# Hybrid decoder trunk: the seven products of a column pair interleaved with those of the next, one weight tile per product, residual added in memory by DMA

## The chip, the core and the metric

The kernel runs on one core of a Trainium2 chip. The metric is the device time of one execution in microseconds (us): the median of three runs, and beside it the time of one execution that the hardware profiler recorded. A core has TensorE (PE, its weight loads PEld), VectorE (DVE), ScalarE (ACT), GpSimd (POOL) and SyncE (SP), each with an in-order queue of its own, and 16 DMA engines that serve the transfers which SP, POOL and ACT issue.

## What is computed

One layer on 2048 tokens of width 1024 in fp32. Three causal mixers share an input and an output projection; behind them stand a gated MLP with a causal convolution of width 3 over the tokens, a per-layer embedding with a gate, and a final RMSNorm. The change lies in the MLP and at its two edges. Cut to that:

```
x = x + y @ w_out                              # y: outputs of the three mixers
h = rmsnorm(x, norm_ffn_gain)
gu = causal_dwconv(h @ ffn_w_up, ffn_conv_w)   # width 3, 2 * 2816 columns
g, u = split(gu, 2)
x = x + (silu(g) * u) @ ffn_w_down             # 2816 -> 1024
gate = sigmoid(x @ ple_w_gate)
x = x + gate * (p @ ple_w_proj)
out = rmsnorm(x, final_norm_gain)
```

## The kernel before

The tokens are worked in two halves of 1024 (`TH`), each of two chunks of 512 (`CH`, `NC` = 2). Features lie on the 128 partitions (`P`), so `x` is eight tiles `x[m]` of 128 x 1024. Each half goes through the mixers, the output projection, the MLP and the embedding; the code is written out in the order in which each engine works it off.

Every fp32 product is three matmuls (`mm3`): each operand is split in a high part, rounded by a copy on ACT (L196), and a low part, the difference taken by DVE (L197). L203 multiplies high by high, L204 the low part of the tokens by high weights, L205 the high tokens by low weights. A matmul takes 128 x 128 weights and 512 tokens.

The MLP has 22 column blocks `j` (`NJ`), each of 128 gate columns (`zg`) and 128 up columns (`zu`). For `j` = 0, `up_first` makes 8 plain products (a product: `KQ` = 4 row blocks of 128, 12 matmuls, one PSUM bank of 128 x 512). For `j` ≥ 1, `up` makes 7 products, a scheme that saves the eighth by sums of weights and of tokens. They are called p1 to p7 after the tokens that they use (`X[1]` to `X[7]`, tiles `h`, split once at the start of the MLP). p1, p6, p7 and p4 accumulate in one bank `pa` (`A`), p5 and p3 in one half of `pbc` (`B`), p2 alone in the other (`Cc`). The running sums are wanted in between, so ACT copies a bank out before the next product adds to it: L849 copies `pa` to `zg` after p1, L857 `pbc` to `zu` after p5, L861 `pa` to `zg` after p6, L894 `pa` to `zu` after p4. Where a product only has to be added to such a copy, DVE does it.

After the products of `j` come the convolutions (`conv_g`, `conv_u`: L344 on ACT, L348 twice on DVE), silu on ACT (L803), the multiply (L808) and the split in `ahi` and `alo` on ACT and DVE. The order of the products is p1, p5, p6, p2, p7, p3, p4 for odd `j` and p1, p2, p5, p6, p3, p7, p4 for even `j`. For even `j`, between the gate's convolution and p4, stands a down-projection group (`down`): two earlier blocks of the activations, times their rows of `w_down`, into all 1024 output features, 16 banks `pdn` of two `j` each (96 matmuls); DVE adds each bank into `x` (L907). The last two blocks follow at the end, one by one. I call two `j` and their group a pair.

Weights arrive on SP's queue as tiles `wr` of 512 KB, two at a time (`wp`), each split by the job that uses it. `w_get` runs the jobs of the list `wlist` two ahead of the one wanted. In the output projection ahead of the MLP GpSimd's queue loads `xr`, the residual, which DVE adds to each bank `po`. For the second half the sums of squares of its `x` are taken ahead of time, during the first half's MLP (`nstats`).

Of the kernel before, what the change touches and what calls it, by code (L numbers as in the profile page):

```python
# [9 lines left out]
F32 = mybir.dt.float32  # L10
# [38 lines left out]
def trunk(ctx, tc, xT, pT, w_in, w_out, w_up, w_down, w_pp, w_pg, wr_bd, wi_bd, vecs, consts, masks, out):  # L49
# [70 lines left out]

    raws = {}

    def job_a(hf, j):
        g = raws[hf, j, 0] = raw_w(kc(w_up[j]))
        raws[hf, j, 1] = raw_w(kc(w_up[NJ + j]))
        hi, lo = ftile("wh", F32R), ftile("wl", F32R)
        split(hi, lo, g)
        return hi, lo

    def job_u(hf, j):  # L130
        hi, lo = ftile("wh", F32R), ftile("wl", F32R)
        split(hi, lo, raws[hf, j, 1])
        return hi, lo

    def job_s(hf, j, which):
        g, u = raws[hf, j, 0], raws[hf, j, 1]
        hi, lo = ftile("wh", F32R), ftile("wl", F32R)
        q = [slice(0, CH), slice(CH, D)]
        if which == 0:

            s = raws[hf, j, 2] = sp.tile([P, D], F32, tag="s", name=nm("s"), bufs=1)
            TT(s[:, q[0]], u[:, q[0]], u[:, q[1]], op=ADD)
            TT(s[:, q[1]], s[:, q[0]], g[:, q[0]], op=SUB)
        else:

            s = raws[hf, j, 2]
            TT(s[:, q[0]], g[:, q[1]], s[:, q[1]], op=SUB)
            TT(s[:, q[1]], g[:, q[0]], u[:, q[0]], op=SUB)
        split(hi, lo, s)
        return hi, lo  # L150

    def job_a22(hf, j):
        t = ftile("w22", F32R)
        split(t[:, :CH], t[:, CH:], raws[hf, j, 1][:, CH:])
        return t

    def job_d(hf, js, m0, per):
        return whole(w_down[m0 : m0 + per, :, js[0] : js[-1] + 1, :].rearrange("m p j c -> p m (j c)"), ftile)
# [3 lines left out]
    for hf in range(NH):  # L162
        wlist += [(("in", hf, m), lambda m=m: whole(kc(w_in[m]), t4)) for m in IN_UNITS]
        wlist += [(("out", hf, c, m), lambda m=m: whole(kc(w_out[m]), t4)) for c in range(NC) for m in range(KD)]
        for j in range(NJ):
            a = (hf, j)
            if j == 0:
                wlist += [(("a", *a), lambda a=a: job_a(*a)), (("u", *a), lambda a=a: job_u(*a))]
                continue
            wlist += [(("a", *a), lambda a=a: job_a(*a))]  # L170
            wlist += [(("s", *a, i), lambda a=a, i=i: job_s(*a, i)) for i in range(2)]
            down = [(("d", hf, j // 2 - 1, i), lambda a=hf, js=GROUPS[j // 2 - 1], i=i: job_d(a, js, 4 * i, 4)) for i in range(2)]
            if j % 2 == 0:
                wlist.append(down[0])
            wlist.append((("a22", *a), lambda a=a: job_a22(*a)))
            if j % 2 == 0:
                wlist.append(down[1])
        wlist += [(("d", hf, gi, 0), lambda a=hf, js=GROUPS[gi]: job_d(a, js, 0, 8)) for gi in range(len(GROUPS) - 2, len(GROUPS))]
        wlist += [(("pg", hf, t, m), lambda m=m: whole(kc(w_pg[m]), t4)) for t in range(len(ple_chunks(hf == NH - 1))) for m in range(KD)]
    wat = {key: i for i, (key, _) in enumerate(wlist)}  # L180
    wmade = {}
    wpos = [0]

    def w_upto(n):
        while wpos[0] < min(n, len(wlist)):
            key, job = wlist[wpos[0]]
            wpos[0] += 1
            wmade[key] = job()

    def w_get(*key, ahead=2):  # L190
        w_upto(wat[key] + 1 + ahead)
        return wmade.pop(key)
# [210 lines left out]
    for hf in range(NH):  # L403
# [291 lines left out]
        pools["ff"] = ff = tc.alloc_tile_pool(name=f"ff{hf}", bufs=9)  # L695


        x = [None] * KD

        def out_evac(c, m, ps, n):  # L700
# [5 lines left out]
            n.add(x[m][:, cks(c)])  # L706

# [77 lines left out]
        def prod(ps, w, xs_, start, stop):  # L785

            for q in range(KQ):
                mm3(ps, (w[0][:, q * P : (q + 1) * P], w[1][:, q * P : (q + 1) * P]), hsl(xs_[q]),
                    start and q == 0, stop and q == KQ - 1, skip_group_check=True)

        def halves(w):
            return [(w[0][:, i * CH : (i + 1) * CH], w[1][:, i * CH : (i + 1) * CH]) for i in range(2)]
# [8 lines left out]
        def conv_g(j, zg):  # L801
            g = conv_gu(j, zg)
            ACT(g, g, AF.Silu)  # L803
            return g

        def conv_u(j, zu, g):
            u = conv_gu(NJ + j, zu)
            TT(g, g, u, op=MUL)  # L808
            hi, lo = t4("ahi", F32R), t4("alo", F32R)
            split(hi, lo, g)  # L810
            acts[j] = (hi, lo)

        def up_first():

            wg, wu = halves(w_get("a", hf, 0)), halves(w_get("u", hf, 0))
            A, A2, BC = ps1(name="pa"), ps1(name="pa"), ps2("pbc")
            zg, zu = ftile("zg"), ftile("zu")
            prod(A, wg[0], X[1], True, False)
            ACT(zg[:, C1], A, AF.Copy)
            norms[1].rstd()  # L820
            prod(A2, wu[0], X[1], True, False)
# [3 lines left out]
            prod(A, wg[1], X[2], False, True)  # L825
            ACT(zg[:, C0], A, AF.Copy)
            next(h2)
            prod(A2, wu[1], X[2], False, True)
            ACT(zu[:, C0], A2, AF.Copy)

            prod(BC[:, C0], wg[0], X[5], True, False)
            prod(BC[:, C1], wu[0], X[5], True, False)
            next(h2)
            prod(BC[:, C0], wg[1], X[3], False, True)
            TT(zg[:, C1], zg[:, C1], BC[:, C0], op=ADD)
            prod(BC[:, C1], wu[1], X[3], False, True)
            TT(zu[:, C1], zu[:, C1], BC[:, C1], op=ADD)
            g = conv_g(0, zg)
            run(h2)
            conv_u(0, zu, g)  # L840

        def up(j, between):
            A, BC = ps1(name="pa"), ps2("pbc")
            B, Cc = BC[:, C0], BC[:, C1]
            zg, zu = ftile("zg"), ftile("zu")

            def p1():
                prod(A, wa[0], X[1], True, False)
                ACT(zg[:, C0], A, AF.Copy)  # L849

            def p2():
                prod(Cc, wa[1], X[2], True, True)
                TT(zg[:, C0], zg[:, C0], Cc, op=ADD)

            def p5():
                prod(B, ws[0], X[5], True, False)
                ACT(zu[:, C1], B, AF.Copy)  # L857

            def p6():
                prod(A, ws[1], X[6], False, False)  # L860
                ACT(zg[:, C1], A, AF.Copy)  # L861

            def p3():
                prod(B, wt[0], X[3], False, True)
                TT(zg[:, C1], zg[:, C1], B, op=ADD)

            def p7():
                prod(A, wt[1], X[7], False, False)
                TT(zu[:, C1], zu[:, C1], A, op=ADD)

            wa = halves(w_get("a", hf, j))
            p1()
            if between is None:
                ws = halves(w_get("s", hf, j, 0))
                p5()
                p6()
                p2()
                wt = halves(w_get("s", hf, j, 1))
                p7()
                p3()  # L880
                g = conv_g(j, zg)
            else:
                p2()
# [197 lines left out]
```

## Time and profile before

| what | us |
|---|---|
| median of 3 runs (2673.24 to 2677.13) | 2676.24 |
| the profiled execution: time | 2678.83 |
| the profiled execution: span, first to last instruction | 2676.7 |
| PE busy (93% of the span) | 2491.7 |
| DVE busy (67%) | 1803.4 |
| ACT busy (42%) | 1130.0 |
| POOL busy (3%) | 91.4 |
| mean granted TensorE clock (1 is full) | 0.975 |
| mixers, half 0 (0 to 381) and half 1 (1340 to 1700) | 381 and 360 |
| output projection (381 to 465, 1700 to 1772) | 84 and 72 |
| MLP (465 to 1215, 1772 to 2537) | 750 and 765 |
| embedding, gate and norm (1215 to 1340, 2537 to the end) | 125 and 139.7 |

The two MLPs are 1515 of 2677 us. The stages overlap by a little; their borders were set by eye, at the change of what TensorE works on. Busy time is the time in which an engine has an instruction in it; a matmul's own duration, 0.39 us, is longer than the distance between two starts, since matmuls are pipelined.

### The profile page before, as it was taken

How to read it: one execution, taken by the hardware profiler on the slowest of the kernel's cores; microseconds unless marked ns; L12 is line 12 of the kernel's file. 1: busy time of each engine (PE TensorE's matmuls, PEld its weight loads, DVE VectorE, ACT ScalarE, POOL GpSimd, SP SyncE). 2: the span in 40 equal slices, each digit the busy share in tenths (PEclk: the TensorE clock that was granted, in tenths of full speed). 3: DMA queues.
4: the chain of work that ended last, by engine and by line, in shares of the span. 5: the costliest groups of instructions: out<-in, count | busy, mean ns of one | idle time of the engine just before them, and what ended most of it. 6: DMA issues, size and time to landing. Idle time of an engine off the chain costs nothing.

```text
span 2676.7 us, 29689 instructions
## 1 busy us (share of the span) xinstructions
PE 2491.7 (93%) x12004; PEld 2023.8 (76%) x12004; DVE 1803.4 (67%) x2530; ACT 1130.0 (42%) x1442; POOL 91.4 (3%) x102
## 2 busy tenths in 40 slices
PE   6999999789999999999999999998999999999998
PEld 4888788577777777777888787876777777777788
DVE  6666566876667777767676656587666666666776
ACT  4344874433333333334444467443333333333253
POOL 2000000200000000000110000020000000000000
PEclk9999999899999999999999999998999999999999
DMA  3111124121111111114321111421111111111143
GB/s 122 40 32 33 40 73 148 60 66 48 48 48 48 48 48 48 54 57 134 134 80 33 32 40 48 130 67 48 46 42 48 48 48 48 48 48 48 55 127 117
DMA packets 73066, 168.94 MB, mean 63 GB/s; under 512 B 5985, under 2 KB 36321, under 8 KB 72929
## 3 DMA queue, kind: packets, MB, share of 16 engines
q1 hardware_dynamic: 66928, 149.08, 17.6%
q0 software_dynamic: 4992, 16.78, 1.9%
q8 instruction: 94, 1.54, 0.3%
q10 hardware_dynamic: 1008, 1.18, 0.2%
q14 instruction: 44, 0.35, 0.0%
HBM read 158.63 MB, written 8.39 MB: 62 GB/s over the span
## 4 chain that ended last, share of the span: by engine, by line
PE 54%; DVE 14%; ACT 9%; issue 2%; DMA 0%; ACTq 0%; DVEq 0%; SPq 0%
PE pdn L203 6%; PE pdn L204 5%; PE pdn L205 5%; DVE gu L348 5%; PE pa L203 3%; PE pbc L203 3%; PE pa L204 3%; PE pa L205 3%; PE pbc L204 3%; PE pbc L205 3%; PE pz L203 2%; PE pz L205 2%; PE pz L204 2%; DVE wl L197 2%; PE pgt L203 2%; PE pgt L205 2%
## 5 line engine op out<-in xcount | busy, mean ns | idle before, releaser
L197 DVE TENSOR_TENSOR wl<-wr,wh 128x1024 fp32r<-128x1024 f32 x210 | 256.2, 1224 | 97.9 <-ACT wh L196 97.7
L203 PE MATMUL pz<-h,wh 128*128 128x512 f32 x768 | 306.9, 400 | 9.6 <-ACT h L196 9.6
L203 PE MATMUL pa<-h,wh 128*128 128x512 f32 x536 | 218.9, 408 | 103.8 <-ACT zg L849 102.3
L907 DVE TENSOR_TENSOR x<-x,pdn 128x512 f32<-128x512 f32 x384 | 255.9, 682 | 82.1 <-PE pdn L205 79.9
L204 PE MATMUL pz<-h,wh 128*128 128x512 f32 x768 | 303.1, 395 | 1.7 <-DVE h L197 1.4
L205 PE MATMUL pz<-h,wl 128*128 128x512 f32 x768 | 301.5, 393 | 0.0
L203 PE MATMUL pdn<-ahi,wh 128*128 128x512 f32 x704 | 279.6, 397 | 10.5 <-DVE x L907 10.5
L205 PE MATMUL pdn<-ahi,wl 128*128 128x512 f32 x704 | 276.2, 392 | 0.0
L204 PE MATMUL pdn<-alo,wh 128*128 128x512 f32 x704 | 276.2, 392 | 0.0
L196 ACT ACTIVATE wh<-wr 128x1024 fp32r<-128x1024 f32 x210 | 218.3, 1052 | 79.3 <-DMA wr<-in_w_down 34.1
L203 PE MATMUL pbc<-h,wh 128*128 128x512 f32 x536 | 219.6, 410 | 15.0 <-ACT zu L857 12.7
L204 PE MATMUL pbc<-h,wh 128*128 128x512 f32 x536 | 215.4, 402 | 4.5 <-DVE h L197 4.5
L205 PE MATMUL pbc<-h,wl 128*128 128x512 f32 x536 | 213.8, 399 | 0.0
L205 PE MATMUL pa<-h,wl 128*128 128x512 f32 x536 | 213.0, 397 | 0.0
L204 PE MATMUL pa<-h,wh 128*128 128x512 f32 x536 | 212.9, 397 | 0.0
L203 PEld LDWEIGHTS pa<-h,wh 128*128 128x128 f32 x536 | 102.8, 192 | 139.4 <-ACT zg L849 117.6
L203 PEld LDWEIGHTS pz<-h,wh 128*128 128x128 f32 x768 | 145.4, 189 | 41.1 <-ACT h L196 10.8
L204 PEld LDWEIGHTS pz<-h,wh 128*128 128x128 f32 x768 | 145.6, 190 | 33.3 <-DVE h L197 4.3
L203 PEld LDWEIGHTS pdn<-ahi,wh 128*128 128x128 f32 x704 | 133.3, 189 | 48.3 <-DVE x L907 21.2
L205 PEld LDWEIGHTS pz<-h,wl 128*128 128x128 f32 x768 | 145.4, 189 | 30.4 <-issue 0.3
L196 ACT ACTIVATE wh<-s 128x1024 fp32r<-128x1024 f32 x84 | 88.2, 1050 | 176.0 <-PE pdn L204 150.9
L348 DVE SCALAR_TENSOR_TENSOR gu<-zu,vt,gu 128x1023 f32<-128x1023 f32 x88 | 112.5, 1278 | 70.2 <-ACT gu L344 70.2
(260 smaller groups left out, 4780.8 us busy)
## 6 DMA issues: line engine op xcount, KB each, us to landing
wr<-in_w_up SPq DMA_DIRECT2D x88, 512.0 KB, 3.7
wr<-in_w_in SPq DMA_DIRECT2D x48, 512.0 KB, 3.7
wr<-in_w_down SPq DMA_DIRECT2D x44, 512.0 KB, 3.8
wr<-in_w_pg SPq DMA_DIRECT2D x40, 512.0 KB, 3.8
wr<-in_w_out SPq DMA_DIRECT2D x32, 512.0 KB, 3.8
xr<-in_xT POOLq DMA_DIRECT2D x32, 256.0 KB, 3.6
out_y<-o SPq DMA_DIRECT2D x24, 256.0 KB, 2.1
xl<-in_xT SPq DMA_DIRECT2D x8, 512.0 KB, 6.2
```

Source lines behind the costliest of these rows:

```text
L196: i = ACT(hi, src, AF.Copy)
L197: last_split[:] = i, (eng or nc.vector).tensor_tensor(lo, src, hi.bitcast(F32), op=SUB)
L203: MM(ps, wk[0], rk[0], start=start, stop=False, **kw)
L204: MM(ps, wk[0], rk[1], start=False, stop=False, **kw)
L205: MM(ps, wk[1], rk[0], start=False, stop=stop, **kw)
L348: STT(dst[:, d:TH], src[:, 0 : TH - d], taps[d], dst[:, d:TH], op0=MUL, op1=ADD)
L907: TT(x[m][:, cks(c)], x[m][:, cks(c)], ps, op=ADD)
```

## The change

Four things change, all in the MLP or at its edges.

- *Order of products.* `up(j)` makes six products, p1, p5, p6, p2, p3, p7; the seventh, p4 of the block before (`last_prod(j - 1)`), stands between p5 and p6. The steps behind it (`u_conv`, `gu_mul`, `gu_split` of `j - 1`) are written out between the products of `j`. p1, p5 and p2 have a bank of their own each (`pa`, `pb`, `pc`, from one pool of four).
- *Weights.* Each product has one tile `wt`, 512 columns of high and 512 of low weights, taken from the pool `bp` of 40 tiles of 128 x 1024, in which `x`, `ahi`, `alo` and the new `st` lie too. Loads and splits are separate jobs: `w_mlp` splits three tiles ahead and loads three further. The loads are of 256 KB: two in a `wr`, or one in a `q`.
- *Residual.* After the output projection `x[m]` is stored in a DRAM tile `xd[m]`. In a group (`down_pair`) ACT copies two banks at once (`pdn`, 128 x 1024) to a tile `st`, and a DMA on GpSimd's queue adds that to `xd[m]` in memory; ahead of the last two blocks `x[m]` is loaded again, and those are added by DVE as before (`down_last`).
- *Statistics of the next half.* They are taken one step a block `j` (`stats_steps`), their loads on SP's queue.

```
-    wp = ctx.enter_context(tc.tile_pool(name="wp", bufs=2))
+    wp = ctx.enter_context(tc.tile_pool(name="wp", bufs=3))
+    dp = ctx.enter_context(tc.tile_pool(name="dp", bufs=1, space=bass.MemoryType.DRAM))
...
+    def one(src):
+
+        t = t4("wt", F32R)
+        split(t[:, :CH], t[:, CH:], src)
         return t
...
+        return [((1, hf, j), load0, lambda: one(raws[a][:, QS[0]])),
+                ((5, hf, j), load1, s1),
+                ((6, hf, j), None, lambda: one(raws[s][:, QS[1]])),
+                ((2, hf, j), None, lambda: one(raws[b][:, QS[1]])),
+                ((3, hf, j), None, s4),
+                ((7, hf, j), None, s3)]
...
+            jobs = up_jobs(hf, j)
+            if j > 1:
+                jobs.insert(2, last_job(hf, j - 1))
+            wlist += jobs
+            if j % 2 == 0 and j:
+                wlist += down_jobs(hf, j // 2 - 1)
...
+    def w_mlp(*key):
+        return w_get(*key, ahead=3, loads=3)
...
-        pools["ff"] = ff = tc.alloc_tile_pool(name=f"ff{hf}", bufs=9)
+        pools["ff"] = ff = tc.alloc_tile_pool(name=f"ff{hf}", bufs=6)
...
             n.add(x[m][:, cks(c)])
+            if c == NC - 1:
+                nc.gpsimd.dma_start(xd[m], x[m])
...
+        def last_prod(j):
+            A, zu = banks.pop(j), zs[j, 1]
+            prod(A, w_mlp(4, hf, j), X[4], False, True)
             ACT(zu[:, C0], A, AF.Copy)
...
+        def up(j):
+            A, B = ps1(name="pa"), ps1(name="pb")
+            banks[j] = A
+            zg, zu = zs[j, 0], zs[j, 1] = ftile("zg"), ftile("zu")
+            prod(A, w_mlp(1, hf, j), X[1], True, False)
+            ACT(zg[:, C0], A, AF.Copy)
+            if j % 2 == 0 or j == 1:
+                g_silu(j - 1)
+            prod(B, w_mlp(5, hf, j), X[5], True, False)
+            ACT(zu[:, C1], B, AF.Copy)
+            if j > 1:
+                last_prod(j - 1)
+            u_conv(j - 1)
+            prod(A, w_mlp(6, hf, j), X[6], False, False)
+            ACT(zg[:, C1], A, AF.Copy)
+            gu_mul(j - 1)
+            Cc = ps1(name="pc")
+            prod(Cc, w_mlp(2, hf, j), X[2], True, True)
+            TT(zg[:, C0], zg[:, C0], Cc, op=ADD)
+            gu_split(j - 1)
+            prod(B, w_mlp(3, hf, j), X[3], False, True)
+            TT(zg[:, C1], zg[:, C1], B, op=ADD)
+            prod(A, w_mlp(7, hf, j), X[7], False, False)
+            TT(zu[:, C1], zu[:, C1], A, op=ADD)
+            g_conv(j)
...
+        def down_pair(gi, todo):
+
             js = GROUPS[gi]
...
+            for m in range(KD):
+                if m % 2 == 0:
+                    w = w_mlp("d", hf, gi, m // 2)
+                ps = ps2("pdn")
                 for c in range(NC):
...
+                st = t4("st")
+                ACT(st, ps, AF.Copy)
+                nc.gpsimd.dma_start(xd[m], st, accum_op=ADD)
+                if m == 0:
+                    todo()
...
         for j in range(1, NJ):
...
+            up(j)
+            if j > 1:
+                next(stats, None)
+            if j % 2 == 0:
+                down_pair(j // 2 - 1, lambda: g_silu(j))
+        run(stats)
+        for m in range(KD):
+            x[m] = t4("x")
+            nc.gpsimd.dma_start(x[m], xd[m])
+        j = NJ - 1
+        g_silu(j)
+        last_prod(j)
+        u_conv(j)
+        gu_mul(j)
+        down_last(len(GROUPS) - 2, lambda: gu_split(j))
+        down_last(len(GROUPS) - 1)
```

The program order of an engine before and after, at the places that matter. `waits X_49` in brackets says that the instruction waits for the semaphore of engine X or of a DMA queue (`DMASW`: issued by GpSimd, `DMAHW`: by SP); each name carries the number of its tile.

TensorE before, around p6 of an odd `j` (p1 of it, twelve rows into `pa_4286`, ends just ahead; the first rows here are the last of p5, then p6 begins):

```order
L203 MATMUL pbc_4287<-h_3409,wh_4220 128x512
L204 MATMUL pbc_4287<-h_3409,wh_4220 128x512
L205 MATMUL pbc_4287<-h_3409,wl_4221 128x512
L203 MATMUL pa_4286<-h_3653,wh_4256 128x512 [waits Activation_49]
L204 MATMUL pa_4286<-h_3653,wh_4256 128x512
L205 MATMUL pa_4286<-h_3653,wl_4257 128x512 [waits DVE_49]
```

TensorE after, around p6 of a later `j` (bank `pa_5086`; the twelve rows of p5 into `pb_5087` stand ahead, and the first rows here are the last of p4 of the block before, into `pa_4786`):

```order
L262 MATMUL pa_4786<-h_3736,wt_5051 128x512
L263 MATMUL pa_4786<-h_3736,wt_5051 128x512
L264 MATMUL pa_4786<-h_3736,wt_5051 128x512
L262 MATMUL pa_5086<-h_3662,wt_5090 128x512 [waits Activation_49]
L263 MATMUL pa_5086<-h_3662,wt_5090 128x512
L264 MATMUL pa_5086<-h_3662,wt_5090 128x512 [waits DVE_49]
```

Between p1 and p6 there were 12 matmuls into another bank, now there are 24.

ACT before, around the copy of p1 (`zg_4698<-pa_4696`) behind a down group:

```order
L803 ACTIVATE gu_4660<-gu_4660 128x1024 [waits DVE_49]
L196 ACTIVATE wh_4700<-s_4668 128x1024 [waits DVE_49]
L849 ACTIVATE zg_4698<-pa_4696 128x512 [waits PE_49]
L196 ACTIVATE ahi_4692<-gu_4660 128x1024 [waits DVE_49]
L196 ACTIVATE wh_4734<-wr_4732 128x1024 [waits DMAHW0_49,PE_49]
```

ACT after, in a down group and at the start of the next `up` (L961 copies two banks to `st`, L255 rounds a weight tile, L924 is the copy of p1):

```order
L961 ACTIVATE st_5460<-pdn_5447 128x1024 [waits PE_49]
L255 ACTIVATE wt_5466<-s_5463 128x512 [waits DMASW0_49,Activation_49]
L961 ACTIVATE st_5482<-pdn_5469 128x1024 [waits DMASW1_49,PE_49,Activation_49]
L961 ACTIVATE st_5498<-pdn_5485 128x1024 [waits PE_49]
L255 ACTIVATE wt_5501<-q_5393 128x512 [waits DMAHW7_49,DMASW2_49,Activation_49]
L961 ACTIVATE st_5517<-pdn_5504 128x1024 [waits DMASW3_49,PE_49,Activation_49]
L961 ACTIVATE st_5533<-pdn_5520 128x1024 [waits PE_49]
L255 ACTIVATE wt_5540<-s_5463 128x512 [waits DMASW4_49,Activation_49]
L255 ACTIVATE wt_5556<-wr_5364 128x512 [waits DMAHW3_49,DMASW5_49,Activation_49]
L255 ACTIVATE wt_5576<-s_5463 128x512 [waits DVE_49]
L924 ACTIVATE zg_5538<-pa_5536 128x512 [waits PE_49]
```

The silu and the split of the activations have left the place around p1's copy, and eight copies to `st` have come in. `DMASW0` to `DMASW5` are the adding transfers of `m` = 0 to 5 of the same group: `st` of `m` = 4 (`st_5482`) waits for that of `m` = 1, `st` of `m` = 6 (`st_5517`) for that of `m` = 3, and weight tiles for those of 0, 2, 4 and 5, since they take the same places of the pool.

GpSimd after, in the output projection (before, only the rows of L762, then L702, stood here, one behind another):

```order
L768 DMA xd_2849<-x_2923 128x1024 [waits DVE_49]
L762 DMA xr_3242<-in_xT 128x512 [waits DMASW6_49,Activation_49]
L768 DMA xd_2850<-x_2932 128x1024 [waits DVE_49]
L762 DMA xr_3297<-in_xT 128x512 [waits DMASW0_49]
L768 DMA xd_2851<-x_2970 128x1024 [waits DVE_49]
```

Each load of `xr` for the second chunk now stands behind a store that waits for DVE's add.

## Rows read from the trace of the kernel before

**Rows 1.** Busy time by stretch: window, us, busy us of each engine, clock, DMA share, GB/s.

```profile
586.38:1171.96 585.58, 551.51 (x2393) 445.73 (x2392) 407.49 (x516) 202.53 (x238) 0.00 (x0) 1.00 0.16 49
1878.52:2492.84 614.32, 565.79 (x2377) 453.86 (x2376) 409.17 (x540) 198.39 (x234) 0.00 (x0) 0.95 0.15 47
```

**Rows 2.** Timeline of PE in the last group of half 0: start, duration, instruction.

```profile
1209.17 0.39 PE L204 MATMUL pdn<-alo,wh 128*128 128x512 f32 x1
1212.57 0.39 PE L204 MATMUL pdn<-alo,wh 128*128 128x512 f32 x1
```

**Rows 3.** Waits of PE in each MLP: total us, times, longest.

```profile
PE pa L203 <- ACT zg L849: 47.2, 20, 11.7
...
PE pa L203 <- ACT zg L849: 55.2, 11, 8.9
```

**Rows 4.** Timeline of PE in one pair of each half; in brackets the wait before.

```profile
717.55 0.39 PE L203 MATMUL pa<-h,wh 128*128 128x512 f32 x1
...
746.65 0.50 PE L203 MATMUL pa<-h,wh 128*128 128x512 f32 x1 [2.62 <-ACT zg L849]
...
782.37 0.39 PE L203 MATMUL pa<-h,wh 128*128 128x512 f32 x1
...
2083.26 0.39 PE L203 MATMUL pa<-h,wh 128*128 128x512 f32 x1
...
2113.68 0.80 PE L203 MATMUL pa<-h,wh 128*128 128x512 f32 x1 [4.62 <-ACT zg L849]
...
2151.53 0.39 PE L203 MATMUL pa<-h,wh 128*128 128x512 f32 x1
```

**Rows 5.** Timeline of ACT ahead of the wait at 2113.68.

```profile
2111.14 1.06 ACT L196 ACTIVATE ahi<-gu 128x1024 fp32r<-128x1024 f32 x1 [4.46 <-DVE gu L808]
2112.11 1.04 ACT L196 ACTIVATE wh<-s 128x1024 fp32r<-128x1024 f32 x1
2113.05 0.58 ACT L849 ACTIVATE zg<-pa 128x512 f32<-128x512 f32 x1
```

**Rows 6.** Groups of DVE in the first MLP: count, busy us, mean ns, idle before.

```profile
L907 DVE TENSOR_TENSOR x<-x,pdn 128x512 f32<-128x512 f32 x179 | 119.5, 683 | 39.8 <-PE pdn L205 39.1
L197 DVE TENSOR_TENSOR wl<-wr,wh 128x1024 fp32r<-128x1024 f32 x45 | 54.9, 1221 | 24.8 <-ACT wh L196 24.8
L197 DVE TENSOR_TENSOR w<-wr,w 128x512 fp32r<-128x512 f32 x21 | 14.4, 688 | 12.3 <-ACT w L196 12.3
```

**Rows 7.** Groups of ACT in the first MLP.

```profile
L196 ACT ACTIVATE wh<-wr 128x1024 fp32r<-128x1024 f32 x44 | 45.4, 1052 | 14.1 <-DMA wr<-in_w_down 13.7 <-DMA wr<-in_w_up 0.4
L196 ACT ACTIVATE w<-wr 128x512 fp32r<-128x512 f32 x21 | 13.0, 619 | 0.0
L849 ACT ACTIVATE zg<-pa 128x512 f32<-128x512 f32 x21 | 12.4, 589 | 31.1 <-DVE gu L348 31.1
```

**Rows 8.** Transfers: queue share, KB and us to landing; all of `xl`.

```profile
q0 software_dynamic: 4992, 16.78, 1.9%
...
xr<-in_xT POOLq DMA_DIRECT2D x32, 256.0 KB, 3.6
xl<-in_xT SPq DMA_DIRECT2D x8, 512.0 KB, 6.2
...
xl<-in_xT POOLq DMA_DIRECT2D x8, 512.0 KB, 5.4
...
DMA to landing us min/median/max: 4.3/5.8/8.5
```

**Rows 9.** Timelines of DVE and PE at the start of each MLP.

```profile
510.73 3.69 DVE L197 TENSOR_TENSOR h<-h,h 128x512 fp32r<-128x512 f32 x6
...
519.36 0.80 PE L203 MATMUL pa<-h,wh 128*128 128x512 f32 x1 [11.68 <-ACT zg L849]
...
524.54 0.50 PE L203 MATMUL pbc<-h,wh 128*128 128x512 f32 x1
...
1814.63 0.79 PE L203 MATMUL pa<-h,wh 128*128 128x512 f32 x1 [8.89 <-ACT zg L849]
```

More of the change, by code (lines that the diff above doesn't have):

```diff
@@ new lines, in last_job, with load, down_jobs @@
+    def last_job(hf, j):
+        def load():
+            raws[hf, j, 3] = raw_q(quarter(j, 1, 1))
+        return (4, hf, j), load, lambda: one(raws[hf, j, 3])
+    def down_jobs(hf, gi):
+        js = GROUPS[gi]
+        per = 4 // len(js)
+        jobs = []
+        for i in range(KD // per):
+            def load(i=i):
+                src = w_down[i * per : (i + 1) * per, :, js[0] : js[-1] + 1, :].rearrange("m p j c -> p m (j c)")
+                raws[hf, gi, "d", i] = raw_q(src)
+            jobs.append((("d", hf, gi, i), load, lambda i=i: one(raws[hf, gi, "d", i])))
+        return jobs
@@ L175, in trunk @@
[L175 to L178, printed above, removed]
+            jobs = up_jobs(hf, j)
[4 more added lines that the diff above has]
+                wlist += down_jobs(hf, j // 2 - 1)
+        wlist.append(last_job(hf, NJ - 1))
@@ L694, in trunk @@
         mx.release()
[L695 removed]
+        pools["ff"] = ff = tc.alloc_tile_pool(name=f"ff{hf}", bufs=6)
         x = [None] * KD
+        xd = [dp.tile([P, TH], F32, name=nm("xd")) for _ in range(KD)]
         def out_evac(c, m, ps, n):
@@ L787, in prod @@
             for q in range(KQ):
[L788 to L792, printed above, removed]
+                mm3(ps, wsl(hsl(w), q), hsl(xs_[q]), start and q == 0, stop and q == KQ - 1, skip_group_check=True)
         C0, C1 = cks(0), cks(1)
@@ new lines, in down_last @@
+        def down_last(gi, todo=None):
+            j = GROUPS[gi][0]
+            w = [w_mlp("d", hf, gi, i) for i in range(2)]
+            for c in range(NC):
+                for m in range(KD):
+                    ps = ps1(name="pdn")
+                    mm3(ps, wsl(hsl(w[m // 4]), m % 4), [a[:, cks(c)] for a in acts[j]], True, True)
+                    TT(x[m][:, cks(c)], x[m][:, cks(c)], ps, op=ADD)
+                    if gi == len(GROUPS) - 1:
+                        xsplit(c, m)
+                    if todo and c == 0 and m == 5:
+                        todo()
@@ L925, in trunk, with stats_steps @@
+        def stats_steps():
+            for c in range(NC):
+                n = Norm()
+                for k in range(KD):
+                    s = t2("xs")
+                    nc.sync.dma_start(s, xT[k, :, T0 + TH + c * CH : T0 + TH + (c + 1) * CH])
+                    n.add(s)
+                    yield
+                n.rstd()
+                nstats.append(n)
         up_first()
+        nstats = []
+        stats = iter(()) if last else stats_steps()
         for j in range(1, NJ):
-            up(j, (lambda gi=j // 2 - 1: down(gi)) if j % 2 == 0 else None)
```

222 lines of the change are left out of this document (90 added, 132 removed).

## The prediction

> **What bounds the kernel now.** I read the stages first, then TensorE's waits, then the timelines around one such wait. In the table of stretches [rows 1] the steady part of the MLP of half 0 (586.38 to 1171.96, nine pairs of `j`) takes 585.58 us, that of half 1 (1878.52 to 2492.84) 614.32 us; the reader should see that PE is busy for 551.51 and 565.79 of them, and that DVE (407.49 and 409.17) and ACT (202.53 and 198.39) are far from full. So PE sets the time, with holes in it. How much the holes cost follows from the beat. At full clock two rows 15 matmuls apart start at 1209.17 and 1212.57 [rows 2], so 3.40/15 = 0.2267 us a matmul, and a product (4 k-tiles x 3) takes 2.72 us. A pair is 2 x 7 products and one down group of 96 matmuls, 264 in all: 59.85 us. Nine are 538.65, so half 0 holds 585.58 − 538.65 = 46.9 us above the beat and half 1 614.32 − 538.65 = 75.7 us: **122.6 us** together.
>
> The list of PE's waits names them: `pa` L203 waits for ACT's `zg` of L849, 47.2 us in 20 waits and 55.2 us in 11 [rows 3]. The rows of one pair in each half show the same: 717.55 to 782.37 is 64.82, with 2.62 of wait at 746.65; 2083.26 to 2151.53 is 68.27, with 4.62 at 2113.68 [rows 4]. After such a wait the matmuls lie further apart: granted clock 0.95 in half 1's stretch, 1.00 in half 0's [rows 1], which is why half 1 holds more above the beat than its waits add up to. That lost clock belongs to the wait and should go with it.
>
> ACT's timeline ahead of 2113.68 shows why the evacuation is late [rows 5]. ACT's queue is in order. `zg` (0.58 us) starts at 2113.05, behind `ahi` at 2111.14, which itself sat 4.46 us for DVE's product `gu` (L808), and behind `wh<-s`. TensorE had finished P1 long before, but P6 accumulates into the same bank, and between the two stands one product (odd `j`), 2.72 us of cover. The convolution, silu, product and split of the pair before stand in the gap and are serial between DVE and ACT.
>
> **The change, part by part.**
>
> *Interleaving.* Between P1 and P6 of `j` now stand P5 of `j` and P4 of `j−1`, 5.44 us; between P6 and P7, which share the bank, P2 and P3, again 5.44. `zg` of P1 is queued on ACT directly behind the product, ahead of the silu, and the u convolution is put after P4, with its multiply and split one and two products further on. So no wait of TensorE hangs on the chain silu–product–`ahi` any more: `acts` of an odd `j−1` are wanted only in the next group, those of an even `j` only a full up pass later. I take the whole 122.6 us as freed, first.
>
> What takes its place is queue work on DVE and ACT inside 59.85 us. DVE loses 16 adds a pair at 0.683 us [rows 6], 10.9 us. Splits of weights become halves: 18 at 0.688 for 8 at 1.221 and 2 at 0.688, 12.4 for 11.1 us, so +1.2. DVE goes from 407.49/9 = 45.3 to some 35.6 us a pair. ACT gains eight copies of a 128x1024 bank pair. That shape from PSUM is in no row: 128x1024 from SBUF takes 1.052, 128x512 from PSUM 0.589 [rows 7], so between 1.05 and 1.18; 8.4 to 9.4 us. Its half splits add 18 x 0.619 − 8 x 1.052 − 2 x 0.619 = 1.5. ACT goes from 202.53/9 = 22.5 to some 33 us. Both fit on average, but about 30 of DVE's 35.6 us fall in the 38.1 us of the 14 products, so a late link can still push one. I found no lasting wait in following the order by hand; for slips I charge 0.5 us a pair, 20 pairs: **+10**. The bounds are 0 and the smaller of the two waits shown, 2.62 us a pair: 52 us.
>
> *Residual in memory.* Eight adding transfers of 512 KB a pair, issued by GpSimd (160 in all, and 8 stores and 8 loads a half around them), replace the adds. GpSimd is idle in both steady stretches [rows 1], so the issue is free. The landing isn't: a staging tile `st` lies in the same ring of 40 tiles as the weight tiles. By the order, `st` of m=4 waits for the transfer of m=1, a weight tile for that of m=2, `st` of m=6 for m=3. Behind such a wait stand all of ACT's later copies, and TensorE's next `pdn` bank waits for those. An `st` is made every 2.72 us, three banks apart, so a landing of up to 7 or 8 us costs nothing. Two such waits follow one another in a group (m=1 on m=4, m=4 on the weights of P6), the second with some slack: walking through the order I get about 1.7 us a pair for each us of landing above 9.
>
> No row shows an adding transfer. The nearest is the 512 KB load on the same queue: 5.4 us median, 4.3/5.8/8.5 least, median and most over both queues [rows 8]. This queue's 16.78 MB kept 16 engines busy 1.9% of the span [rows 8]: 50.9 us for 32 times 512 KB, 1.6 us each, against one every 2.72. The value that I take is 5 to 7 us (5.4, up to 1.6 more if the old value is read as a transfer of its own): hidden, cost 0. The ends are 4.3 (0) and 8.5 x 2 = 17 us, if the read and the write of the old sum are each a slow transfer.
>
> The Trainium skill ("Collectives: The Full Stack", section "The bandwidth ceiling: the fold count and why AG ≠ RS ≠ AR") says that a transfer that adds reads two sources and that these reads share one ring, so that it moved 62.28/32.35 = 1.93 times less in its case; no run before this one shows that here. By that rule the estimate is 1.6 x 1.93 = 3.1 us each against the 2.72 spacing, and the sum would be some 25 us higher.
>
> *Start of each MLP.* P6 of `j`=1 waits 11.68 us to 519.36, and the product after it starts at 524.54, 5.18 us for 12 matmuls against 2.72: 2.5 us of slow clock [rows 3, 9]. DVE ends the last split of `h` at 510.73 + 3.69 = 514.4 [rows 9]. The weights of `j`=1 are now split behind that work, so I start its 21 products (7 and 6 of the two `j`, the down group as 8; P4 of `j`=2 comes later) at 515: 515 + 57.1 + 2.5 = 574.6, against 586.38 − 2.72 = 583.7, a gain of 9. By the same shift of 519.4 − 515 = 4.4, half 1 resumes at 1814.6 − 4.4 = 1810.2 [rows 9]: 1810.2 + 59.6 = 1869.8 against 1878.52 − 2.72 = 1875.8: 6. **−15.** Bounds: 0, if the splits of `h` and weights tread on each other, and 24, if P1 and P5 of `j`=1 run ahead as now.
>
> *Edges.* In the output projection each 256 KB load of `xr` (3.6 us, [rows 8]) is now queued on GpSimd behind the store of `xd` that waits for DVE: about 1 us a half, **+2**. The 8 reloads of `x` at the end of each MLP are issued once the last adds have landed, while the last up pass (7 products, 19 us) still runs: 8 x 1.6 = 12.8 us on the engines, hidden; for the tail **+2**. Without that cover it would be 6 to 13 us a half.
>
> *Sum.* The profiled execution took 2678.8 us (span 2676.7), 2.6 above the median 2676.24. 2678.8 − 122.6 − 15 + 10 + 2 + 2 = 2555.2.
>
> **Rivals.**
>
> A, the forecast: adds land in under 8 us, the queues keep up. For it: the 5.4 us row and an idle queue. 2555, from 2535 (no slips, 122.6 + 15 + 6 off) to 2590 (slips of 2.2 us a pair).
>
> B, the adding transfers back up. If each keeps the engines twice as long as a load, 2 x 1.6 = 3.2 us against the 2.72 between two of them, the eighth is 8 x 0.48 = 3.8 us late and lands after 6 + 3.8 = 9.8; ACT then waits 1.7 x 0.8 = 1.4 us a pair, 27 us: 2582. At a landing of 11.5 us it is 4.3 a pair, 85 us: 2640. For it: the old sum must be read from somewhere; against: in two thirds of a pair no such transfer runs. 2580 to 2650. The rule of the Trainium skill named above would bring this about.
>
> C, the other side: slower than before. With 122.6 + 15 − 14 = 123.6 us to lose over 20 pairs, 6.2 us a pair, and 1.7 us a pair for each us, the change breaks even at a landing of 9 + 6.2/1.7 = 12.6 us. At 15 us it costs 10.2 a pair, 2555 + 204 = 2759. For it: 8.5 us has been seen for a plain load, and a sum needs a read and a write; against: no 512 KB row has a median above 6.2 [rows 8]. Some 2680 to 2770.
>
> D, the waits only move: DVE's 30 us inside 38.1 are in order, and P7 of each `j`, the weight split and the convolution alternate between DVE and ACT. If each pair still loses 2.6 to 5 us, 2600 to 2660.
>
> **How the numbers follow.** Chances: A 0.58, B 0.20, C 0.12, D 0.10. Likeliest: A, 2555, its own range 2535 to 2590. A, B and D hold 0.88 between 2535 and 2660; I end at 2650 and start at 2535, which leaves C and the edges out. About 0.2% (5 us) is what a measurement of this kernel tells from no change. Faster holds A, B, D less the parts of B and D that could run past 2650, and a little of C below break-even: 0.83; same 0.03; slower 0.14.
>
> **What would show it.** Right: the wait of `pa` for `zg` drops below 10 us in all; a pair takes 60 to 60.5 us in both halves, at a granted clock of 0.99 or more; the adding transfers land in 5 to 7 us; the copies of `st` wait for PE alone. Step on slips wrong: PE waits for a weight tile's split or for P7's bank. Landing wrong: ACT's `st` or weight copies wait for a DMA, PE waits for `pdn` banks, and pairs reach 62 us (B) or over 66 (C). Wrong most of all would be a landing over 10 us, since every term but the first is small.

## The result and the profile after

The changed kernel takes 2551.43 us (median of 4, 2548.32 to 2553.68) against 2676.68 for the kernel before in the same comparison: a ratio of 0.9527, 95% interval 0.9504 to 0.9551. The prediction said 2555. The profiled execution took 2548.32 us, span 2546.5, mean granted clock 0.987.

Busy time by stretch of the kernel after: the nine steady pairs of each half, from P1 of `j` = 3 to P1 of `j` = 21 as before (columns as in [rows 1]).

```profile
579.11:1121.63 542.52, 541.97 (x2393) 447.32 (x2392) 320.33 (x444) 283.45 (x384) 61.87 (x73) 1.00 0.57 131
1826.88:2365.44 538.56, 538.56 (x2378) 446.25 (x2376) 324.89 (x468) 279.89 (x378) 61.58 (x72) 1.00 0.58 132
```

585.58 became 542.52 and 614.32 became 538.56 [rows 1]; PE is busy all the time. The beat of 264 matmuls makes 538.65, so of the 122.6 us above it 118.8 are gone. DVE went from 407.49 to 320.33 (35.6 us a pair, as reckoned), ACT from 202.53 to 283.45 (31.5 a pair; 33 were reckoned), and the clock of half 1 rose from 0.95 to 1.00.

TensorE's waits over the whole program of the kernel after; the lines of the MLP and its edges, the longest first:

```profile
PE pm L313 <- DVE sq L305: 14.7, 2, 12.2
PE pdn L262 <- DVE x L974: 11.0, 4, 4.9
...
PE pbc L262 <- DVE zg L905: 8.5, 2, 6.7
PE pa L264 <- DVE wt L256: 6.8, 2, 3.7
...
PE pdn L262 <- ACT st L961: 1.4, 2, 1.0
```

The 102.4 us for `zg` [rows 3] aren't there any more; what is left comes once or twice a half, at the edges. The timeline of PE shows the beat itself, P1 of two odd blocks in each half:

```profile
579.11 0.39 PE L262 MATMUL pa<-h,wt 128*128 128x512 f32 x1
...
638.95 0.39 PE L262 MATMUL pa<-h,wt 128*128 128x512 f32 x1
...
1826.88 0.39 PE L262 MATMUL pa<-h,wt 128*128 128x512 f32 x1
...
1886.72 0.39 PE L262 MATMUL pa<-h,wt 128*128 128x512 f32 x1
```

59.84 us both times, against 64.82 and 68.27 [rows 4]. ACT's timeline around the copy of P1 (L924), in the kernel after:

```profile
661.02 1.06 ACT L867 ACTIVATE gu<-gu 128x1024 f32<-128x1024 f32 x1 [3.20 <-DVE gu L407]
661.99 0.58 ACT L924 ACTIVATE zg<-pa 128x512 f32<-128x512 f32 x1
662.47 1.14 ACT L255 ACTIVATE wt<-s 128x512 fp32r<-128x512 f32 x2
...
672.07 1.06 ACT L255 ACTIVATE ahi<-gu 128x1024 fp32r<-128x1024 f32 x1 [2.39 <-DVE gu L874]
```

Where [rows 5] had `ahi` and a weight split of 1.04 us in front of `zg`, `ahi` now comes 10 us behind it. The silu (L867), which the code now has behind the copy, hasn't left this place everywhere: here, as in ten other blocks, it stands directly in front of the copy. So, other than I said of the kernel before, an engine doesn't always work off its instructions in the order of the code. The adding transfers: count and median landing (us) from the list of transfers, the copy that feeds them from the groups, and their least, median and longest landing.

```profile
xd<-st POOLq DMA_DIRECT2D x160, 512.0 KB, 6.1
...
L961 ACT ACTIVATE st<-pdn 128x1024 f32<-128x1024 f32 x160 | 164.0, 1026 | 210.5 <-PE pdn L264 189.9
...
DMA to landing us min/median/max: 5.2/6.1/9.2
```

6.1 us, inside the 5 to 7 taken. ACT's copy is 1.03 us, below the 1.05 to 1.18 that were bounds. One of the signs of being right failed: the copies to `st` don't wait for PE alone, but 11 times for an adding transfer, 20.5 us in all (the row is shown with e4 and e8). TensorE waits 1.4 us for `st` over the whole program.

### The profile page after: what moved, and what is told of

Same layout as the page of the kernel before. It is cut to its first block, busy times and chain, and to the rows that moved or that the text cites. A ratio compares the mean times of both kernels' runs of the same rounds, so it can differ in the third digit from the quotient of the medians.

```text
span 2546.5 us, 30816 instructions
## 1 busy us (share of the span) xinstructions
PE 2454.9 (96%) x12004; PEld 2020.1 (79%) x12004; DVE 1613.4 (63%) x2384; ACT 1310.7 (51%) x1778; POOL 237.2 (9%) x278
## 3 DMA queue, kind: packets, MB, share of 16 engines
q0 software_dynamic: 31360, 113.26, 21.3%
q10 hardware_dynamic: 1008, 1.18, 0.2%
## 5 line engine op out<-in xcount | busy, mean ns | idle before, releaser
L262 PE MATMUL pdn<-ahi,wt 128*128 128x512 f32 x704 | 277.7, 394 | 12.6 <-DVE x L974 11.0
L264 PE MATMUL pa<-h,wt 128*128 128x512 f32 x704 | 276.5, 393 | 6.8 <-DVE wt L256 6.8
L262 PE MATMUL pa<-h,wt 128*128 128x512 f32 x704 | 276.3, 393 | 3.3 <-ACT wt L255 1.8
L263 PE MATMUL pdn<-alo,wt 128*128 128x512 f32 x704 | 275.8, 392 | 0.0
L264 PE MATMUL pdn<-ahi,wt 128*128 128x512 f32 x704 | 275.6, 392 | 0.0
L263 PE MATMUL pa<-h,wt 128*128 128x512 f32 x704 | 275.6, 391 | 0.0
L961 ACT ACTIVATE st<-pdn 128x1024 f32<-128x1024 f32 x160 | 164.0, 1026 | 210.5 <-PE pdn L264 189.9
L256 DVE TENSOR_TENSOR wt<-s,wt 128x512 fp32r<-128x512 f32 x168 | 114.1, 688 | 218.0 <-ACT wt L255 217.8
L962 POOL DMA_DIRECT2D xd<-st x160 | 136.9, 856 | 1087.4 <-ACT st L961 1084.3
L262 PEld LDWEIGHTS pdn<-ahi,wt 128*128 128x128 f32 x704 | 133.2, 189 | 45.6 <-DVE x L974 13.9
L256 DVE TENSOR_TENSOR wl<-wr,wh 128x1024 fp32r<-128x1024 f32 x120 | 146.2, 1227 | 35.1 <-ACT wh L255 34.7
L264 PEld LDWEIGHTS pa<-h,wt 128*128 128x128 f32 x704 | 133.3, 189 | 35.3 <-DVE wt L256 7.7
L262 PEld LDWEIGHTS pa<-h,wt 128*128 128x128 f32 x704 | 133.1, 189 | 33.0 <-ACT wt L255 2.7
L264 PEld LDWEIGHTS pdn<-ahi,wt 128*128 128x128 f32 x704 | 133.2, 189 | 28.0
L263 PEld LDWEIGHTS pa<-h,wt 128*128 128x128 f32 x704 | 133.1, 189 | 27.6
L263 PEld LDWEIGHTS pdn<-alo,wt 128*128 128x128 f32 x704 | 133.3, 189 | 27.1
```

The lines of the kernel that those rows point to most:

```text
L256: last_split[:] = i, (eng or nc.vector).tensor_tensor(lo, src, hi.bitcast(F32), op=SUB)
L262: MM(ps, wk[0], rk[0], start=start, stop=False, **kw)
L263: MM(ps, wk[0], rk[1], start=False, stop=False, **kw)
L264: MM(ps, wk[1], rk[0], start=False, stop=stop, **kw)
L961: ACT(st, ps, AF.Copy)
L962: nc.gpsimd.dma_start(xd[m], st, accum_op=ADD)
```

## The experiments

Each was compared with the kernel before on the same chip. I held two theories from the start: the interleaving takes the waits away (theory 1), or VectorE's freed time and the smaller weight tiles do. A third came out of the runs.

**e1: VectorE copies the banks.**

```
-                ACT(st, ps, AF.Copy)
+                nc.vector.tensor_copy(st, ps)
```

> The changed kernel, but VectorE instead of ScalarE copies each pair of banks to the staging tile, so VectorE has about as much work a pair as in the kernel before (eight copies of 128x1024, some 1.2 to 1.4 us each, 10 to 11 us). Theory 1 (the order of the products took the waits away, VectorE has slack in the down groups): within 10 us of the changed kernel, 2548 to 2562 us. Rival (the time that the adds gave back to VectorE carries the gain): 2 to 3 us a pair come back, 2590 us or more.

2553.2 us, ratio 0.9531 (0.9517 to 0.9545): no different from the change. DVE's copies take 1.223 us each, 9.8 us a pair, so it is about as busy as in the kernel before, and it costs nothing: the copies fall into the down group, where DVE has time left (it stands idle for 152.3 us ahead of these copies, until TensorE has filled a bank). What the adds gave back to VectorE isn't what pays.

```profile
L961 DVE COPY st<-pdn 128x1024 f32<-128x1024 f32 x160 | 195.7, 1223 | 152.3 <-PE pdn L264 152.3
```

**e2: P4 of the block before moved behind P6.**

```
-                jobs.insert(2, last_job(hf, j - 1))
+                jobs.insert(3, last_job(hf, j - 1))
...
-            if j > 1:
-                last_prod(j - 1)
-            u_conv(j - 1)
             prod(A, w_mlp(6, hf, j), X[6], False, False)
             ACT(zg[:, C1], A, AF.Copy)
+            if j > 1:
+                last_prod(j - 1)
+            u_conv(j - 1)
             gu_mul(j - 1)
```

> The changed kernel with the seventh product of the block before moved from in front of P6 to behind it: one product (2.72 us) between P1 and P6, as for an odd block of the kernel before; the steps behind it still run between the products. Theory 1a (what counts is that ScalarE's queue is free when P1 ends; its copy takes 0.6 us): one product is cover enough, 0 to 25 us more than the changed kernel, 2550 to 2575 us. Theory 1b (the distance of two products is needed): 1 to 3 us at every P6, 42 of them: 2595 to 2680 us.

2564.6 us, but spread from 2553.5 to 2573.3; ratio 0.957 (0.9541 to 0.9599). The trace, of the fastest run, has 3.7 us of waits for the copy of P1 in all; what spreads the runs stays open. One product of cover is nearly enough. The 5.44 us between P1 and P6, the core of my argument, isn't what removes the wait.

**e3: interleaving undone, the rest of the change kept.**

```
+            if j % 2 == 0 or j == 1:
+                g_silu(j - 1)
+            if j > 1:
+                last_prod(j - 1)
+            u_conv(j - 1)
+            gu_mul(j - 1)
+            gu_split(j - 1)
             prod(A, w_mlp(1, hf, j), X[1], True, False)
             ACT(zg[:, C0], A, AF.Copy)
...
```

(the same calls are taken out further down, and P4's weights are made ahead of P1's)

> The changed kernel with the interleaving undone and all else kept: the seventh product of the block before, its convolution, multiply and split are written ahead of P1. Theory 1 (interleaving took the waits away): at least half of the 119 us come back, 2610 to 2670 us, and TensorE's waits for the copy of P1 return. Rival (the freed VectorE time and the smaller weight tiles do it): under 2575 us.

2596.0 us, ratio 0.9692 (0.9678 to 0.9706). It lies between the two: 45 us came back, not 60 or more. And they are not the old wait. TensorE's waits in e3, the two longest of this kind:

```profile
PE pa L262 <- ACT wt L255: 24.6, 2, 13.1
PE pc L262 <- ACT wt L255: 15.5, 20, 3.1
```

It waits for weight tiles (twice at the starts of the MLPs, and 0.8 us at each of 20 products P2), never for the copy of P1. So without any interleaving, and with one product between P1 and P6, the old wait is gone. Theory 1 falls as a whole; something else in the change had already removed it.

**e6: the kernel before with the residual in memory alone.** The copies are of one bank each.

```
-            TT(x[m][:, cks(c)], x[m][:, cks(c)], ps, op=ADD)
+            if c == 0:
+                sts[0] = t4("st")
+            ACT(sts[0][:, cks(c)], ps, AF.Copy)
+            if c == NC - 1:
+                nc.gpsimd.dma_start(xd[m], sts[0], accum_op=ADD)
```

(and the stores and reloads of `x`)

> The kernel before with one part of the change alone: the residual kept in memory, ScalarE copying each bank (128x512) to a staging tile and GpSimd's queue adding it in memory. Theory 1: TensorE still waits for the copy of P1, 2640 to 2690 us, perhaps slower than before since ScalarE's queue holds 16 more copies a pair. Rival (freeing VectorE is what shortens the chain): 2.5 us a pair or more saved, under 2620 us.

2694.7 us, ratio 1.006 (1.0043 to 1.0077): 16 us slower than before. The wait is whole:

```profile
PE pa L204 <- ACT zg L853: 102.1, 31, 10.8
```

**e9 and e10: the weight jobs of the kernel before, with and without interleaving.** In both, the changed kernel gets back the jobs of two products each, two ahead, with their sums (`job_a`, `job_s`, `job_a22`, `job_d`). These weight tiles lie in a pool of 11 other tiles, and the ring has 38 without them. e10 also moves P4 and its steps ahead of P1 as in e3.

```
-        return w_get(*key, ahead=3, loads=3)
+        return w_get(*key, ahead=2)
...
-            prod(A, w_mlp(1, hf, j), X[1], True, False)
+            wa = halves(w_mlp('a', hf, j))
+            prod(A, wa[0], X[1], True, False)
```

> The changed kernel, interleaved, with the weight jobs of the kernel before: a high and a low tile of 128x1024 for two products, the sums taken in the same job, two jobs ahead, loads not ahead (ring 38, 11 other tiles). Theory 2 (the wait came from the copy of P1 standing behind a whole weight job on ScalarE, whose sums stand behind convolutions on VectorE; two products of cover don't hide all of that): 2590 to 2640 us. Rival (interleaving alone is enough, as the prediction had it): 2550 to 2575 us.

> Both undone: the weight jobs of the kernel before, and the seventh product and its steps ahead of P1; what stays of the change is the residual in memory and the order and banks of the other six products. Theory 2: the waits are back, 2660 to 2710 us, as in the kernel before with the residual in memory. Rival (the order or the banks of the six products carry much of the gain): under 2630 us.

e9: 2564.2 us, ratio 0.956 (0.953 to 0.9589). e10: 2546.9 us, ratio 0.9503 (0.9482 to 0.9523). Both expectations of theory 2 fail. e9 alone would fit its rival, that interleaving is enough, but e10 takes that away: with neither interleaving nor the new weight tiles it is as fast as the change. TensorE's list in e10 has 11.9 us left for the copy of P1:

```profile
PE pa L242 <- ACT zg L914: 11.9, 3, 6.1
```

The four runs together: with the new weight tiles interleaving saves 45 us (2596.0 to 2551.4), with the old ones it costs 17 (2546.9 to 2564.2; TensorE waits 15.0 us for `st` in e9 and 2.6 in e10). It repairs what the smaller tiles need, no more.

**e11: the kernel before with two lines swapped.** e6 and e10 differ in the order of the six other products and in their banks. The odd blocks of the kernel before ran P7 ahead of P3.

```
                 wt = halves(w_get("s", hf, j, 1))
-                p7()
                 p3()
+                p7()
                 g = conv_g(j, zg)
```

> The kernel before with two lines swapped: in odd blocks the third product is written ahead of the seventh, as it already is in even blocks and as the changed kernel has it in all. The gate's convolution needs the third product and not the seventh, so the chain convolution, silu, product, split can start one product (2.72 us) earlier. Theory 3 (the wait of the even blocks' P6 comes from that chain standing on VectorE's and ScalarE's queues in front of the copy of P1; 2.72 us earlier shortens it by as much): the waits of 2.6 us in half 0 and 4.6 in half 1 shrink to 0 and 2 a pair, with their slow clock 50 to 100 us saved, 2580 to 2630 us. Rival (the gain needs the freed VectorE time or the other banks as well): within 20 us of the kernel before, 2660 to 2690 us.

2602.6 us, ratio 0.9705 (0.9681 to 0.9728): **78 us of the 125 from two lines.** The gate's convolution needs P3 and not P7. ACT's timeline in e11 ahead of P6 of an even block, at the place of [rows 5]:

```profile
2130.36 1.04 ACT L196 ACTIVATE wh<-s 128x1024 fp32r<-128x1024 f32 x1
2132.41 0.60 ACT L849 ACTIVATE zg<-pa 128x512 f32<-128x512 f32 x1 [1.00 <-PE pbc L204]
...
2135.54 1.06 ACT L196 ACTIVATE ahi<-gu 128x1024 fp32r<-128x1024 f32 x1 [0.24 <-DVE gu L808]
```

and P6 itself, from PE's timeline:

```profile
2133.06 0.50 PE L203 MATMUL pa<-h,wh 128*128 128x512 f32 x1 [0.46 <-ACT zg L849]
```

The wait of 4.62 us is 0.46. ACT now waits for TensorE at the copy, not for VectorE ahead of it. That is more than the 2.72 us of the earlier start: the code still has `ahi` of the odd block ahead of the copy, but in ACT's queue it has gone behind it. The copy is released by a row of P2 (`pbc` L204), the last but one, so some wait is left. All pairs but one are 62.9 to 63.0 us in both halves, 3 above the beat. Two short waits at the shared bank `pbc` are part of what is left:

```profile
PE pbc L203 <- ACT zu L857: 12.3, 21, 0.8
...
PE pbc L203 <- DVE zg L853: 3.4, 11, 0.3
```

**e12: the kernel before with the order and the banks of the change.**

```
-            A, BC = ps1(name="pa"), ps2("pbc")
-            B, Cc = BC[:, C0], BC[:, C1]
+            A, B = ps1(name="pa"), ps2("pb")[:, C0]
+            Cc = ps2("pc")[:, C0]
...
-                p7()
                 p3()
+                p7()
...
-                p2()
                 ws = halves(w_get("s", hf, j, 0))
                 p5()
                 p6()
+                p2()
```

> The kernel before with the order P1, P5, P6, P2, P3, P7, P4 for all blocks and tiles of their own in PSUM for the fifth and the second product; its weight jobs, its residual in SBUF with VectorE's adds, and its seventh product at its own place stay. It is the kernel e10 without the residual in memory. Theory 3 (order and banks of the products carry the gain): 2545 to 2570 us. Rival (the 55 us between e11 and e10 come from the residual in memory, which takes 11 us a pair from VectorE): 2590 to 2610 us, as e11.

2549.0 us, ratio 0.951 (0.9497 to 0.9523), the whole gain, with the residual in SBUF, the old weight jobs and P4 at its old place. TensorE's waits for the copy of P1 there:

```profile
PE pa L203 <- ACT zg L849: 5.0, 5, 2.0
```

Of e11's remaining 53 us, how much goes to the even blocks' order and how much to the banks wasn't tried apart. Both waits at the shared bank are gone here, which speaks for the banks but doesn't price them.

**e4 and e8: what a late landing costs.** e4 adds each staging tile twice, the first time to a second set of tiles; e8 takes two tiles out of the ring.

```
+                nc.gpsimd.dma_start(xe[m], st, accum_op=ADD)
                 nc.gpsimd.dma_start(xd[m], st, accum_op=ADD)
```

```
-    bp = ctx.enter_context(tc.tile_pool(name="bp", bufs=40))
+    bp = ctx.enter_context(tc.tile_pool(name="bp", bufs=38))
```

> The changed kernel with each staging tile added twice in memory, the first time into a second set of memory tiles that nobody reads: 16 adding transfers a pair. Theory (landing is hidden only while it stays under some 8 us; each add keeps the engines 2.9 us, so two a bank are 5.8 against a bank every 2.72, and the queue backs up within a group): landings grow to 12 to 25 us, copies and weight tiles wait for tiles of the ring, 5 to 15 us a pair, 2650 to 2850 us. Rival (there is ample slack): under 2580 us.

> The changed kernel with 38 in place of 40 tiles in the ring that weight tiles, activations and staging tiles share. Theory (a staging or weight tile waits for the adding transfer that last held its place; landing is 6.1 us against a limit of about 8 with 8 free places): with 6 free places the limit falls to some 3 to 5 us, and 1.5 to 4 us a pair appear as waits of ScalarE for these transfers, 2580 to 2640 us. Rival (places are not short): within 5 us of the changed kernel.

e4: 2717.4 us, ratio 1.0129 (1.0106 to 1.0152), slower than the kernel before. e8: 2605.0 us, ratio 0.9711 (0.969 to 0.9732). Both as the theory of the ring says: ACT waits for transfers. ACT's waits in e4, in e8 and in the change:

```profile
ACT wt L255 <- DMA xd<-st: 153.7, 63, 5.1
ACT st L963 <- DMA xd<-st: 147.9, 40, 6.0
...
ACT st L961 <- DMA xd<-st: 218.4, 96, 4.9
...
ACT st L961 <- DMA xd<-st: 20.5, 11, 2.9
```

Landing in e4 and in e8 (least, median, longest):

```profile
DMA to landing us min/median/max: 5.1/8.3/11.4
...
DMA to landing us min/median/max: 5.0/5.4/9.0
```

Landing is counted from GpSimd's issue, and in e4 the issue itself comes late. GpSimd's timeline in e4, in the middle of a group:

```profile
2126.28 0.87 POOL L965 DMA_DIRECT2D xd<-st  x1 [1.64 <-issue]
2128.76 0.86 POOL L964 DMA_DIRECT2D xe<-st  x1 [1.61 <-issue]
2131.24 0.84 POOL L965 DMA_DIRECT2D xd<-st  x1 [1.62 <-issue]
```

From there on one add goes out every 2.5 us or more, where two are wanted every 2.72. From the end of a copy to the landing of its last add, when its place in the ring is free, e4's trace has a median of 19.0 us (6.5 in the change, 5.8 in e8), though the median landing is 8.3. So the queue does back up, to the 12 to 25 us expected, but ahead of the issue. Of the 166 us that this costs, 118 fall into the 18 steady pairs, 6.5 a pair. e8 pays 54 us with its places free in 5.8 us: there it is the number of places that is short.

**e5: a plain store in place of the add.**

```
-                nc.gpsimd.dma_start(xd[m], st, accum_op=ADD)
+                nc.gpsimd.dma_start(xd[m], st)
```

> The changed kernel with a plain store in place of each adding transfer, so that the sums of the ten groups are left out and only the last stays. Theory (an add reads twice, its landing is hidden): landing falls from 6.1 to 3 to 4 us, the queue's time on the engines from about 2.9 to 1.6 us each, and the whole time stays within 5 us of the changed kernel. Rival (the adds' landing still costs something): 10 us or more faster.

2547.7 us, ratio 0.9492 (0.9476 to 0.9507), some 4 us below the change: the adds are all but free. The queue's share of the engines in e5 and after, and the landing in e5:

```profile
q0 software_dynamic: 31360, 113.26, 11.7%
...
q0 software_dynamic: 31360, 113.26, 21.3%
...
DMA to landing us min/median/max: 2.9/2.9/5.3
```

**e7: the last splits of the tokens ahead of the first convolution.**

```
-            g_conv(0)
             run(h2)
+            g_conv(0)
```

> The changed kernel with the last splits of the tokens written ahead of the first convolution at the start of each MLP. Theory (the start gained 5 us instead of 15 since the last splits end 4 us later than before, behind the convolution): 4 to 9 us faster than the changed kernel, 2542 to 2548 us. Rival (the order of VectorE is set by what is ready, or the weights of the next block are late anyway): within 2 us.

2552.5 us, ratio 0.9511 (0.9494 to 0.9528): nothing gained. P1's third matmul, the first that needs low weights, runs 1.5 us earlier than in the change (519.36, below), and a wait of 3.39 us in the first down group takes it back:

```profile
517.84 0.69 PE L264 MATMUL pa<-h,wt 128*128 128x512 f32 x1 [2.30 <-DVE wt L256]
...
573.67 0.80 PE L262 MATMUL pdn<-ahi,wt 128*128 128x512 f32 x1 [3.39 <-ACT st L961]
```

## Why the prediction was right, and where it wasn't

**The sum.** The steady pairs were to give 122.6 − 10 = 112.6 us and gave 118.8: the slips were 3.8 us in all, not 10, all in half 0. Everything outside the steady stretches was to give 15 − 4 = 11, and went from 2676.7 − 1199.90 = 1476.8 to 2546.5 − 1081.08 = 1465.4 us, 11.4. That this fits is in part luck: with the P4 that now comes later counted alike, it is 4.6 us ahead of the steady pairs of half 0 (9 were reckoned), 1.3 between the two stretches and 5.5 behind the last, where a loss of 2 was reckoned.

**The cause was wrong.** The excess was rightly found, rightly priced and rightly expected to vanish, with its slow clock. The failed step is the first sentences of *Interleaving*: that P6 waited because one product was too little cover, and that P5 with P4 of the block before supplies it. The rows already spoke against it. The wait at 2113.68 [rows 4] is in an even block, and in the code of an even block two products, P2 and P5, stand between P1 and P6; only odd blocks have one. In TensorE's queue the first three matmuls of P6 come between P2 and P5. The last row of P1, the last of P2 and the first of P5 there:

```profile
2105.95 0.39 PE L205 MATMUL pa<-h,wl 128*128 128x512 f32 x1
...
2108.67 0.39 PE L205 MATMUL pbc<-h,wl 128*128 128x512 f32 x1
...
2115.24 0.80 PE L203 MATMUL pbc<-h,wh 128*128 128x512 f32 x1
```

P1 ends at 2106.3 and its copy at 2113.05 + 0.58 = 2113.6 [rows 5], 7.3 us later: 5.44 us of products would not have covered that. One product is enough in e3 and nearly in e2, and e12 has the whole gain without interleaving. Nor did the steps of the block before have to be written behind P1, the other half of *Interleaving*: the code of e10 and e12 has them ahead.

What the runs show in its place: the gate's convolution of an odd block waited for P3, the last product ahead of it; the chain convolution, silu, product, split then stood on VectorE's and ScalarE's queues in front of the copy of P1 of the even block. With P3 one product earlier the wait shown is 0.46 in place of 4.62 us and the kernel 78 us faster (e11); with the order and the banks the whole gain is there (e12). I had read that queue off [rows 5] and then argued from the distance between P1 and P6. I had also listed P3 ahead of P7 as part of the new order without asking what P3 releases. The price of the wait needed no cause, only the beat; that the change took the wait away was luck as far as my cause goes, since it also held the order and the banks, in which I had seen no gain.

**Side by side, the parts of the change nearly cancel.** On the kernel before, the residual in memory alone costs 16 us (e6). It takes VectorE from 407.49 to 317.54 us in the steady pairs of half 0, and these hardly change: 582.71 and 614.48 us in the two halves against 585.58 and 614.32, so the loss lies outside them. Beside the new order it costs nothing: e10 has it, e12 hasn't, at 2546.9 and 2549.0 us (they also differ in the statistics of the next half and the sizes of the pools). The small weight tiles cost TensorE waits, and interleaving pays them back (e3). e12, with neither, runs most of its pairs in 60.8 to 61.4 us instead of 59.84 and is as fast over all. The steady stretches of e12, from P1 of `j` = 3 to P1 of `j` = 21:

```profile
567.86:1123.56 555.70, 549.56 (x2393) 444.44 (x2392) 408.32 (x519) 203.48 (x240) 0.54 (x1) 1.00 0.17 53
1818.52:2366.61 548.09, 546.29 (x2377) 443.20 (x2376) 407.56 (x540) 198.46 (x234) 0.00 (x0) 1.00 0.17 52
```

They take 22.7 us more than the change's, and e12 makes up for it outside: its first stretch begins at 567.86 instead of 579.11, and 694.96 us lie between the two instead of 705.25. So the change loses ahead of the first stretch and between the two what it gains in the pairs.

**The start of the MLP.** The products of `j` = 1 were to run from 515. The first two matmuls of P1 ran at 513.88, the third waited for the low weights. DVE and PE in the kernel after:

```profile
514.41 4.29 DVE L256 TENSOR_TENSOR h<-h,h 128x512 fp32r<-128x512 f32 x7
...
519.36 0.80 PE L264 MATMUL pa<-h,wt 128*128 128x512 f32 x1 [3.18 <-DVE wt L256]
```

The last splits of `h` end at 518.7 instead of 514.4 [rows 9], and PE resumes at 519.36, 4.4 us late. Gain of half 0: 583.66 − 579.11 = 4.6, half of the 9 reckoned. Putting the splits first didn't help (e7): VectorE has no gap over 0.23 us there from 494 to 522.

**The rivals.** A came true. B's mechanism is real but weaker than priced: by e5, an add keeps the engines (21.3% x 2546.5 − 11.7% x 2546.0)/160 = 1.53 us longer than a store of the same bytes, and the store itself takes 1.35 (the queue's 297.9 us less 38.2, over its 192 further transfers; the 38.2 are three quarters of the 50.9 of the kernel before, since a quarter of those bytes now comes by SP's queue): 2.9 us an add, 2.1 times the store. The Trainium skill's rule ("Collectives: The Full Stack", section "The bandwidth ceiling: the fold count and why AG ≠ RS ≠ AR"), that an add reads twice, agrees in kind, with its factor of 1.93. But 2.9 against the 2.72 between two adds doesn't back up by much in eight: in one group of half 1 the landings grow from 5.4 to 7.7 us. C's price was wrong on both sides. In e4 the places come free 19.0 us behind the copy; 1.7 us a pair for each us above 9 would make 17 a pair, and 6.5 were measured. In e8 they come free in 5.8 us, where the price is nothing, and two places fewer cost 54 us. C's break-even of 12.6 us is not shown: e4 is slower than the kernel before at 19.0, and no run lies between that and the 8.2 of e10. The change stands nearer to that edge than its 1.4 us of PE waits for `st` lets one see. D didn't happen: a pair of half 1 takes the beat, 59.84 us.

## What to carry to other kernels

The size of a stall can be read off the beat without knowing its cause, but the cause can't be read off the distance between two products: ask which product releases the chain that stands in the queue ahead of the late instruction, and put that product first. Before a rebuild, try its smallest piece alone: here two swapped lines gave 78 of 125 us, and the order with the banks gave all of it, with the residual left where it was. When several parts of a change arrive together, a two-by-two of them costs three more runs and shows which part only repairs another.

## What the hardware showed that I had not expected

The adding transfers land nearly as fast as a plain load of the same size did (6.1 us, and 5.4 for `xl` [rows 8]); a store from the same tiles lands in 2.9 (e5). They keep the engines twice as long as a store (2.9 and 1.35 us each), and 160 of them cost some 4 us in all. Wanted faster than one in 2.5 us, they wait at GpSimd's issue, where the time to landing doesn't show it (e4: 8.3 us to landing, 19.0 from the copy). The kernel's time is also more exposed to two tiles of a ring than to the transfers' own speed: 54 us for the one, 4 for the other.
